# Four moves in a decoder trunk's order of work: first joint weights, weight sums, a shared sum, norm matmuls

## The chip, the cores and the metric

The kernel runs on one core of a Trainium2 chip, in one launch. The metric is device time in microseconds. Of the kernel before there are three timed runs, median 2136.77 (2134.54 to 2140.83), and one profiled execution, whose own time is 2129.51.

## The reference

Two decoder layers on `x[1, 1024, 1024]`, all in float32. Each layer is

```python
    for layer in range(DEPTH):
        h = _rmsnorm(x, pre_mix_g[layer])
        # layer 0: Conformer convolution and RG-LRU side by side; layer 1: mLSTM
        h = mixer(h)
        x = x + _rmsnorm(h, post_mix_g[layer])
        h = _swiglu(_rmsnorm(x, pre_ffn_g[layer]), w_gate[layer], w_up[layer], w_down[layer])
        x = x + _rmsnorm(h, post_ffn_g[layer])

def _swiglu(xn, w_gate, w_up, w_down):
    g = jnp.einsum('bsd,df->bsf', xn, w_gate)
    up = jnp.einsum('bsd,df->bsf', xn, w_up)
    return jnp.einsum('bsf,fd->bsd', jax.nn.silu(g) * up, w_down)
```

with a model width of 1024 and a feed-forward width of 2816 (22 blocks of 128). The Conformer branch of layer 0 holds a layer norm over 512 channels; two of its matmuls per half form the mean and the variance.

## The kernel before, in words

**Products.** To keep float32 accuracy, each operand is split in two float32r tiles, `hi` (a cast on ScalarE, L131) and `lo` (the rest, a subtraction on VectorE, L132), and each product is three matmuls: hi by hi, hi by lo, lo by hi (`mm3`, L125 to L128). A matmul has a 128x128 stationary tile and 512 moving columns. The sequence is worked on in two halves, A and B, of 512 rows.

**Feed-forward with seven products.** Class `Ffn` computes the two halves of both matrix products as a 2x2 block product in seven instead of eight block products, so it needs sums and differences of operand blocks. `phase0` and `down_first` (product d1) need half A alone. `phase1` does for each of 11 pairs of blocks `m` the products that need both halves: `pa`, `pb`, `pc`, each for gate and up. Their weights come from `prep1`: two loads of gate (`ri`, `rj`), two of up, four subtractions for each on GpSimd (L448 to L451: `t14`, `t23`), then the splits `t2.`, `t1.` and `b22`. The operands `s2`, `s3` are made from the features of half B (`feature_b`, names `xs2`, `xs3`), and a rest of twelve splits (`feature_c`: `xs1`, `xa22`, `xs4`) follows the first weights. `phase2` then does the products of `w_down`: d2, d3, d6, d5, d7 and a last one, each of 11 rounds (`down`); a round loads two 128x512 blocks into one raw tile, casts it (`whid`), subtracts (`wlod`) and issues 12 matmuls. The weights of d6 and of the products behind it are sums, made in `down_sums`: for each of the 11 pairs four loads (`wq`), four subtractions on GpSimd (`wt`) and four stores (`ft`).

**Sandwich.** After each mixer and feed-forward the residual step runs as a side generator (`sandwich`): for each of four row blocks a sum of squares, a power on GpSimd (`srp..`, `srn..`, L147), multiplications on VectorE (L214, L216), a store, and then the transposes that feed `feature_b`.

**What sets the order.** The code is a set of generators that are advanced in turn by given paces, and the list scheduler of the language then reorders the instructions of each engine; so where an edit lands is seen only in the order of the built program. Every engine works its own row of instructions in order. All loads and stores are issued by SyncE (SP), also in order: an issue that waits for a buffer holds the ones behind it. Buffers: 5 raw tiles shared by all weight loads, 4 `hi` and 4 `lo` tiles, 30 units, 13 small tiles, 8 banks of PSUM.

Names carry the layer and the pair: `whit200g` is the cast of `t2`, layer 0, pair 0, gate; `wlod0s31` is the subtraction of layer 0, product with `s3`, round 1. A number behind an underscore in an order row only numbers the tile.

Of the kernel before, what the change touches and what calls it, by code (L numbers as in the profile page):

```python
# [12 lines left out]
OP = mybir.AluOpType  # L13

P = 128
D = 1024
S = 1024
T = 512
NT = 4
# [21 lines left out]
def trunk(ctx: ExitStack, tc: tile.TileContext, x, w_in, w_out, w_gate, w_up, w_down,  # L41
# [18 lines left out]
    def ps_main(name):  # L60
        return pp.tile([P, T], F32, tag="mm", name=name, bufs=4)

    def ps_aux(shape, name):
        return pp.tile(shape, F32, tag="aux", name=name, bufs=4)
# [258 lines left out]
    TT = nc.vector.tensor_tensor  # L323

    class Ffn:
# [103 lines left out]
        def prep1(self, m):  # L429
            return self.prep1b(m, *self.prep1a(m))  # L430

        def prep1a(self, m):
            l = self.l
            sub = nc.gpsimd.tensor_tensor
            res = []
            raw = []
            for kind in range(2):
                name = f"{l}{m}{'gu'[kind]}"
                ri = raw_tile([P, D], f"ri{name}")
                rj = raw_tile([P, D], f"rj{name}")  # L440
                src = (w_gate, w_up)[kind]
                nc.sync.dma_start(ri, src[l, m])
                nc.sync.dma_start(rj, src[l, m + HP])
                u2 = small([P, T], f"u2{name}")
                nc.sync.dma_start(u2, self.d_p[m, kind])
                t23 = unit([P, 2, T], F32, f"t23{name}")
                t14 = unit([P, 2, T], F32, f"t14{name}")
                sub(t14[:, 0], rj[:, 0:T], ri[:, 0:T], op=OP.subtract)  # L448
                sub(t23[:, 0], rj[:, T:], t14[:, 0], op=OP.subtract)
                sub(t23[:, 1], rj[:, T:], rj[:, 0:T], op=OP.subtract)  # L450
                sub(t14[:, 1], ri[:, T:], t23[:, 0], op=OP.subtract)  # L451
                raw.append((rj, t23, t14))
                res.append({"u2": u2})
            for kind in range(2):
                u = unit([P, 2, T], F32R, f"b22{l}{m}{'gu'[kind]}")
                split(u[:, 0], u[:, 1], raw[kind][0][:, T:])
                res[kind]["b22"] = (u[:, 0], u[:, 1])
            return res, raw
# [13 lines left out]
        def phase1(self, ms):  # L472
            l = self.l
            ms = list(ms)
            w_next = self.prep1(ms[0])
            for _ in self.rest:
                pass
            for n, m in enumerate(ms):
                w, h11 = w_next
                u2 = [w[k]["u2"] for k in range(2)]  # L480
# [113 lines left out]
        def down_first(self):  # L594

            a = [ps_main(f"d1{self.l}{t}") for t in range(NT)]
            for _ in self.down(a, "a11", (0, 0), True):
                yield 2.8
            for t in range(NT):
                f = small([P, T], f"y1{self.l}{t}")  # L600
                nc.scalar.copy(f, a[t])
                nc.sync.dma_start(self.d_y[t], f)

        def phase2(self, oa, ob, by_t=False):
# [5 lines left out]
            u2 = [small([P, T], f"v2{l}{t}") for t in range(NT)]  # L610
            for t in range(NT):
                nc.sync.dma_start(u2[t], self.d_y[t])
            for _ in self.down_sums():
                pass
            a = [ps_main(f"d2{l}{t}") for t in range(NT)]
            for _ in self.down(a, "a12", (1, 0), True):
                yield 2.8
            for t in range(NT):
                TT(ya[t][:, lo], a[t], u2[t], op=OP.add)
            b = [ps_aux([P, T], f"d3{l}{t}") for t in range(NT)]  # L620
            for _ in self.down(b, "s4", (1, 1), True):
                yield 2.8
            for t in range(NT):
                nc.scalar.copy(ya[t][:, hi], b[t])  # L624
            a = [ps_main(f"d6{l}{t}") for t in range(NT)]
# [7 lines left out]
            for t in range(NT):  # L633
                nc.scalar.copy(yb[t][:, hi], b[t])
                TT(ya[t][:, hi], b[t], ya[t][:, hi], op=OP.add)
                TT(ya[t][:, hi], ya[t][:, hi], u2[t], op=OP.add)
                oa.ready = t
            a = [ps_main(f"d7{l}{t}") for t in range(NT)]
            for _ in self.down(a, "s3", "t3", True):
                yield 2.8  # L640
            for t in range(NT):
                TT(yb[t][:, hi], a[t], yb[t][:, hi], op=OP.add)
                TT(yb[t][:, hi], yb[t][:, hi], u2[t], op=OP.add)
            for t in self.down(a, "a22", "t4", False, by_t):
                if t is not None:
                    TT(yb[t][:, lo], a[t], u2[t], op=OP.add)
# [161 lines left out]
    def conformer(m):  # L808
# [16 lines left out]
        sq = [q[j // 2][:, j % 2] for j in range(4)]  # L825

        def mean(src, tmp, name):
            pm = ps_aux([P, T], name)
            nc.gpsimd.tensor_tensor(tmp[0], src[0], src[1], op=OP.add)
            nc.vector.tensor_tensor(tmp[2], src[2], src[3], op=OP.add)  # L830
            nc.vector.tensor_tensor(tmp[0], tmp[0], tmp[2], op=OP.add)
            nc.tensor.matmul(pm, onesl, tmp[0], start=True, stop=True)
            return pm

        pm = mean(acc, sq, f"pm{h}")
        yield
        for j in range(4):
            nc.vector.tensor_tensor(acc[j], acc[j], pm, op=OP.subtract)
            nc.scalar.activation(sq[j], acc[j], AF.Square)
            yield  # L840
        pv = mean(sq, sq, f"pv{h}")
        yield
        rs = sq[3]
        nc.scalar.activation(rs, pv, AF.Sqrt, bias=epsc)
        nc.vector.reciprocal(rs, rs)
# [378 lines left out]
    ob = Out("oB")  # L1224
    gb = start(sandwich(ob, x, x1, post_mix[0:1], 1, gf(0), f0.feature_b, 6), 1.0)
    run(Project(mb.yT, ob, OUT0).run())
    run(f0.phase0(LATE))
    run(f0.down_first())
    drain(gb)
# [22 lines left out]
    pb = Out("pB")  # L1252
    gb = start(sandwich(pb, x2, x3, post_mix[1:2], 1, gf(1), f1.feature_b, 6), 1.0)
    run(Project(nb.yT, pb, OUT1).run())
    run(f1.phase0(LATE))
    run(f1.down_first())
    drain(gb)
# [96 lines left out]
```

## Time and profile before

| what | value |
|---|---|
| median of three runs | 2136.77 us (2134.54 to 2140.83) |
| profiled execution, its own time | 2129.51 us |
| its span in the trace | 2127.7 us |
| mean granted clock of TensorE | 0.990 |
| TensorE (PE) busy | 2049.7 us, 96% |
| VectorE (DVE) busy | 1455.5 us, 68% |
| ScalarE (ACT) busy | 925.9 us, 44% |
| GpSimd (POOL) busy | 704.7 us, 33% |
| chain that ended last | PE 67%, DVE 13%, DMA 9%, issue 6%, ACT 4% |

The span runs from the first to the last instruction of the trace; the 1.8 us by which the time is longer lie around it. [...] Busy shares are means over the whole span: the stages differ, and each is to be read by itself.

### The profile page before, as it was taken

To read this page: it belongs to the slowest core of one execution; us is meant where nothing else is said; L and a number is where in the kernel's file an instruction comes from. 1 tells how busy PE (TensorE), PEld (TensorE's weight loads), DVE (VectorE), ACT (ScalarE), POOL (GpSimd) and SP (SyncE) were. 2 spreads that over 40 slices of the span, in tenths; PEclk is the share of its full clock that TensorE was granted. 3 is DMA by queue.
4 is the path that set the end of the run, shared out by engine and by line. 5 is a ranking of instruction groups with operands and counts; after the bars stand their busy time and mean duration, and the time that the engine had idled before them with its cause. 6 is when DMAs were issued, how large, how long until landed. Compare 5 with 4: busy or idle time off the path is not lost.

```text
span 2127.7 us, 26147 instructions
## 1 busy us (share of the span) xinstructions
PE 2049.7 (96%) x9200; PEld 1669.0 (78%) x9200; DVE 1455.5 (68%) x2017; ACT 925.9 (44%) x1313; POOL 704.7 (33%) x473
## 2 busy tenths in 40 slices
PE   7998989997999999999999999999997999999998
PEld 6776867785888887878988887778885888888786
DVE  7998479569677776567643755556469877777567
ACT  5666477654222222445343334555454222223353
POOL 4454554627444336401000000300016643445310
PEclk9999999998999999999999999999998999999999
DMA  6232544475454459966563653756464545469966
GB/s 229 92 117 81 182 163 163 144 248 187 164 167 160 168 201 366 342 203 229 190 208 118 219 180 99 257 179 213 134 223 176 192 167 168 165 214 367 327 225 220
DMA packets 202740, 417.39 MB, mean 196 GB/s; under 512 B 19920, under 2 KB 48720, under 8 KB 202608
## 3 DMA queue, kind: packets, MB, share of 16 engines
q1 hardware_dynamic: 202608, 415.72, 57.2%
q8 instruction: 72, 1.18, 0.2%
q14 instruction: 60, 0.49, 0.1%
HBM read 302.82 MB, written 112.82 MB: 195 GB/s over the span
## 4 chain that ended last, share of the span: by engine, by line
PE 67%; DVE 13%; DMA 9%; issue 6%; ACT 4%; POOL 1%; SPq 1%; DVEq 0%; POOLq 0%; ACTq 0%
PE pb L128 4%; PE pb L126 4%; PE pb L127 4%; PE pc L128 3%; PE pc L126 3%; PE pc L127 3%; DVE pcv L754 3%; PE d L126 3%; PE d L127 3%; PE d L128 3%; PE p L126 3%; PE p L127 3%; PE p L128 3%; DMA ft<-wt 2%; PE pa L128 2%
## 5 line engine op out<-in xcount | busy, mean ns | idle before, releaser
L107 ACT CAST whi<-raw 128x1024 fp32r<-128x1024 f32 (+2 forms) x164 | 164.3, 1006 | 244.2 <-PE p L127 50.0
L109 POOL TENSOR_TENSOR wlo<-raw,whi 128x1024 fp32r<-128x1024 f32 x66 | 162.0, 2461 | 165.8 <-ACT whi L107 126.5
L109 DVE TENSOR_TENSOR wlo<-raw,whi 128x1024 fp32r<-128x1024 f32 (+2 forms) x98 | 111.7, 1145 | 123.7 <-ACT whi L107 122.8
L754 DVE SCALAR_TENSOR_TENSOR pcv<-cy,vec,pcv 128x512 f32<-128x512 f32 x240 | 172.1, 749 | 4.4 <-ACT pcv L751 1.6
L1091 POOL TENSOR_TENSOR hrr<-hss,half 128x8 f32<-128x8 f32 x8 | 13.1, 1643 | 243.7 <-DVE hss L1089 243.7
L132 DVE TENSOR_TENSOR wlod1s<-r21s,whid1s 128x1024 fp32r<-128x1024 f32 x44 | 58.5, 1334 | 46.4 <-ACT whid1s L131 46.0
L132 DVE TENSOR_TENSOR wlod0s<-r20s,whid0s 128x1024 fp32r<-128x1024 f32 x44 | 57.6, 1310 | 44.0 <-ACT whid0s L131 39.8
L126 PE MATMUL p<-xTnoA,whi 128*128 128x512 f32 x176 | 71.8, 412 | 6.2 <-ACT gel L729 2.6
L131 ACT CAST whid1s<-r21s 128x1024 fp32r<-128x1024 f32 x44 | 46.4, 1054 | 66.7 <-PE d L128 38.0
L131 ACT CAST whid0s<-r20s 128x1024 fp32r<-128x1024 f32 x44 | 46.4, 1054 | 61.3 <-PE d L128 49.0
L127 PE MATMUL d<-wlod0s,whid0s 128*128 128x512 f32 x176 | 69.2, 393 | 2.0 <-DVE wlod0s L132 2.0
L126 PE MATMUL p<-xTnpA,whi 128*128 128x512 f32 x176 | 70.9, 405 | 0.0
L127 PE MATMUL p<-xTnoA,whi 128*128 128x512 f32 x176 | 70.3, 400 | 0.0
L128 PE MATMUL p<-xTnpA,wlo 128*128 128x512 f32 x176 | 70.3, 401 | 0.0
L127 PE MATMUL p<-xTnpA,whi 128*128 128x512 f32 x176 | 70.1, 399 | 0.0
L128 PE MATMUL p<-xTnoA,wlo 128*128 128x512 f32 x176 | 69.8, 400 | 0.0
L128 PE MATMUL d<-whid1s,wlod1s 128*128 128x512 f32 x176 | 69.1, 393 | 0.0
L127 PE MATMUL d<-wlod1s,whid1s 128*128 128x512 f32 x176 | 69.0, 392 | 0.0
L128 PE MATMUL d<-whid0s,wlod0s 128*128 128x512 f32 x176 | 68.6, 390 | 0.0
L126 PE MATMUL d<-whid1s 128*128 128x512 f32 x176 | 63.1, 394 | 3.1 <-ACT yeA L624 3.1
L132 DVE TENSOR_TENSOR wlod0a<-r20a,whid0a 128x1024 fp32r<-128x1024 f32 x33 | 47.3, 1440 | 25.3 <-ACT whid0a L131 23.8
L548 POOL TENSOR_TENSOR wt<-wq 128x512 f32<-128x512 f32 x22 | 34.7, 1575 | 89.0 <-DMA wq<-in_w_down 49.6
(2484 smaller groups left out, 6640.8 us busy)
## 6 DMA issues: line engine op xcount, KB each, us to landing
wq<-in_w_down SPq DMA_DIRECT2D x88, 256.0 KB, 5.1
ft<-wt SPq DMA_DIRECT2D x88, 256.0 KB, 5.1
raw<-in_w_in SPq DMA_DIRECT2D x32, 512.0 KB, 3.4
raw<-in_m_in SPq DMA_DIRECT2D x32, 512.0 KB, 4.9
raw<-in_w_gate SPq DMA_DIRECT2D x22, 512.0 KB, 4.5
raw<-in_w_up SPq DMA_DIRECT2D x22, 512.0 KB, 3.6
fp<-p1f SPq DMA_DIRECT2D x44, 256.0 KB, 2.5
fs<-s SPq DMA_DIRECT2D x44, 256.0 KB, 3.5
```

The source lines that it names most:

```text
L107: nc.scalar.copy(hi[:, 0:n], raw[:, 0:n])
L109: eng.tensor_tensor(lo[:, 0:n], raw[:, 0:n], hi[:, 0:n].bitcast(F32), op=OP.subtract)
L126: nc.tensor.matmul(ps, l[0], r[0], start=first, stop=False, **kw)
L127: nc.tensor.matmul(ps, l[0], r[1], start=False, stop=False, **kw)
L128: nc.tensor.matmul(ps, l[1], r[0], start=False, stop=last, **kw)
L131: nc.scalar.copy(dst_hi, src)
L132: nc.vector.tensor_tensor(dst_lo, src, dst_hi.bitcast(F32), op=OP.subtract)
L548: sub(t[0][:, 0], q[0][:, 1], q[0][:, 0], op=OP.subtract)
L754: nc.vector.scalar_tensor_tensor(dst, src[:, k:k + T], V(wname, w0 + k), dst, op0=OP.mult, op1=OP.add)
L1091: nc.gpsimd.tensor_tensor(rr, ss, half, op=OP.pow)
```

## The change

Four edits, in both layers except the last.

1. `prep1a` can be called for gate and up apart, and splits `b22` of each right away. The gate part of the first pair is called ahead of `phase0(LATE)`, that is ahead of the last first-half pair; the up part after the fourth round of `down_first`. `phase1` then only calls `prep1b` for it.
2. `phase2` no longer runs all of `down_sums` ahead of d2: one pair's sums are issued in every second round of d2 and d3, and the rest behind.
3. The add of the shared sum `u2` to the upper half of `yb` moves from behind product d7 to ahead of it.
4. In the layer norm of layer 0 the two `mean` matmuls of each half are emitted four steps of the generator later, after their sums.

```diff
-        def prep1a(self, m):
+        def prep1a(self, m, kinds=(0, 1), begun=None):
...
-            res = []
-            raw = []
-            for kind in range(2):
+            res, raw = begun or ([], [])
+            for kind in kinds:
...
                 res.append({"u2": u2})
-            for kind in range(2):
                 u = unit([P, 2, T], F32R, f"b22{l}{m}{'gu'[kind]}")
                 split(u[:, 0], u[:, 1], raw[kind][0][:, T:])
...
-            w_next = self.prep1(ms[0])
+            w_next = self.prep1b(ms[0], *self.begun)
...
-            for _ in self.down(a, "a11", (0, 0), True):
+            for i, _ in enumerate(self.down(a, "a11", (0, 0), True)):
                 yield 2.8
+                if i == 3:
+                    self.begun = self.prep1a(0, (1,), self.begun)
...
-            for _ in self.down_sums():
-                pass
+            sums = self.down_sums()
             a = [ps_main(f"d2{l}{t}") for t in range(NT)]
-            for _ in self.down(a, "a12", (1, 0), True):
+            for i, _ in enumerate(self.down(a, "a12", (1, 0), True)):
+                if i % 2 == 0:
+                    next(sums, None)
                 yield 2.8
...
-            for _ in self.down(b, "s4", (1, 1), True):
+            for i, _ in enumerate(self.down(b, "s4", (1, 1), True)):
+                if i % 2 == 0 or i == 9:
+                    next(sums, None)
                 yield 2.8
+            for _ in sums:
+                pass
...
                 oa.ready = t
+            for t in range(NT):
+                TT(yb[t][:, hi], yb[t][:, hi], u2[t], op=OP.add)
             a = [ps_main(f"d7{l}{t}") for t in range(NT)]
...
                 TT(yb[t][:, hi], a[t], yb[t][:, hi], op=OP.add)
-                TT(yb[t][:, hi], yb[t][:, hi], u2[t], op=OP.add)
...
         def mean(src, tmp, name):
-            pm = ps_aux([P, T], name)
...
+            for _ in range(4):
+                yield
+            pm = ps_aux([P, T], name)
             nc.tensor.matmul(pm, onesl, tmp[0], start=True, stop=True)
+            yield
             return pm
...
+    f0.begun = f0.prep1a(0, (0,))
     run(f0.phase0(LATE))
...
+    f1.begun = f1.prep1a(0, (0,))
     run(f1.phase0(LATE))
```

What the scheduler makes of it, at three places. First POOL's row in layer 0 around the last two row blocks of the sandwich (`srp`, `srn`) and the first pair's subtractions (`t14`, `t23`); before:

```order
L147 TENSOR_TENSOR srpoB2_3558<-svpoB2_3556,half_78 128x1
L147 TENSOR_TENSOR srnoB2_3582<-svnoB2_3580,half_78 128x1
L147 TENSOR_TENSOR srpoB3_3592<-svpoB3_3590,half_78 128x1
L147 TENSOR_TENSOR srnoB3_3630<-svnoB3_3628,half_78 128x1
L448 TENSOR_TENSOR t1400g_4021<-rj00g_4015,ri00g_4014 128x512
L450 TENSOR_TENSOR t2300g_4020<-rj00g_4015 128x512
L449 TENSOR_TENSOR t2300g_4020<-rj00g_4015,t1400g_4021 128x512
L448 TENSOR_TENSOR t1400u_4033<-rj00u_4027,ri00u_4026 128x512
L450 TENSOR_TENSOR t2300u_4032<-rj00u_4027 128x512
L451 TENSOR_TENSOR t1400g_4021<-ri00g_4014,t2300g_4020 128x512
```

and of the changed kernel:

```order
L147 TENSOR_TENSOR srpoB2_3558<-svpoB2_3556,half_78 128x1
L447 TENSOR_TENSOR t1400g_3602<-rj00g_3596,ri00g_3595 128x512
L449 TENSOR_TENSOR t2300g_3601<-rj00g_3596 128x512
L448 TENSOR_TENSOR t2300g_3601<-rj00g_3596,t1400g_3602 128x512
L147 TENSOR_TENSOR srnoB2_3582<-svnoB2_3580,half_78 128x1
L147 TENSOR_TENSOR srpoB3_3592<-svpoB3_3590,half_78 128x1
L450 TENSOR_TENSOR t1400g_3602<-ri00g_3595,t2300g_3601 128x512
L147 TENSOR_TENSOR srnoB3_3645<-svnoB3_3643,half_78 128x1
L447 TENSOR_TENSOR t1400u_3891<-rj00u_3885,ri00u_3884 128x512
L449 TENSOR_TENSOR t2300u_3890<-rj00u_3885 128x512
```

The gate subtractions moved in among the sandwich's powers, and the up subtractions follow the last power. Layer 1 has the same rows with `pB` for `oB`.

Second, DVE's row in `phase2` of layer 1, around the adds that read the product d2 (`d21.`, L619, in the changed kernel L620) among the splits of d3 (`s4`) and d6 (`s2`); before:

```order
L132 TENSOR_TENSOR wlod1s20_16142<-r21s20_16138,whid1s20_16141 128x1024
L132 TENSOR_TENSOR wlod1s21_16161<-r21s21_16157,whid1s21_16160 128x1024
L132 TENSOR_TENSOR wlod1s22_16180<-r21s22_16176,whid1s22_16179 128x1024
L132 TENSOR_TENSOR wlod1s23_16199<-r21s23_16195,whid1s23_16198 128x1024
L619 TENSOR_TENSOR yeA0_15508<-d210_15700,v210_15516 128x512
L619 TENSOR_TENSOR yeA1_15509<-d211_15701,v211_15517 128x512
```

and of the changed kernel:

```order
L132 TENSOR_TENSOR wlod1s40_15845<-r21s40_15841,whid1s40_15844 128x1024
L132 TENSOR_TENSOR wlod1s41_15880<-r21s41_15876,whid1s41_15879 128x1024
L620 TENSOR_TENSOR yeA0_15508<-d210_15524,v210_15516 128x512
L132 TENSOR_TENSOR wlod1s42_15899<-r21s42_15895,whid1s42_15898 128x1024
L620 TENSOR_TENSOR yeA1_15509<-d211_15525,v211_15517 128x512
```

The adds stood behind the fourth split of d6 and stand now behind the second of d3, 13 splits earlier.

Third, DVE's row in layer 0 between the products d5 and d7 (`d50.` is d5's sum, `v20.` the shared sum); before:

```order
L635 TENSOR_TENSOR yfA0_6316<-d500_7163,yfA0_6316 128x512
L635 TENSOR_TENSOR yfA1_6317<-d501_7164,yfA1_6317 128x512
L635 TENSOR_TENSOR yfA2_6318<-d502_7165,yfA2_6318 128x512
L636 TENSOR_TENSOR yfA0_6316<-yfA0_6316,v200_6324 128x512
L635 TENSOR_TENSOR yfA3_6319<-d503_7166,yfA3_6319 128x512
L636 TENSOR_TENSOR yfA1_6317<-yfA1_6317,v201_6325 128x512
L636 TENSOR_TENSOR yfA2_6318<-yfA2_6318,v202_6326 128x512
L132 TENSOR_TENSOR wlod0s31_7425<-r20s31_7421,whid0s31_7424 128x1024
```

and of the changed kernel:

```order
L640 TENSOR_TENSOR yfA0_6316<-d500_7163,yfA0_6316 128x512
L644 TENSOR_TENSOR yfB0_6320<-yfB0_6320,v200_6324 128x512
L640 TENSOR_TENSOR yfA1_6317<-d501_7164,yfA1_6317 128x512
L644 TENSOR_TENSOR yfB1_6321<-yfB1_6321,v201_6325 128x512
L640 TENSOR_TENSOR yfA2_6318<-d502_7165,yfA2_6318 128x512
L644 TENSOR_TENSOR yfB2_6322<-yfB2_6322,v202_6326 128x512
L641 TENSOR_TENSOR yfA0_6316<-yfA0_6316,v200_6324 128x512
L640 TENSOR_TENSOR yfA3_6319<-d503_7166,yfA3_6319 128x512
L644 TENSOR_TENSOR yfB3_6323<-yfB3_6323,v203_6327 128x512
L641 TENSOR_TENSOR yfA1_6317<-yfA1_6317,v201_6325 128x512
L132 TENSOR_TENSOR wlod0s31_7429<-r20s31_7425,whid0s31_7428 128x1024
```

Seven adds stood ahead of the split of the second round of d7, and ten stand there now.

## Rows read from the trace of the kernel before

**Rows 1.** The page, busy us, share of the span, instructions.

```profile
PE 2049.7 (96%) x9200; PEld 1669.0 (78%) x9200; DVE 1455.5 (68%) x2017; ACT 925.9 (44%) x1313; POOL 704.7 (33%) x473
```

**Rows 2.** PE's waits, whole span: us in total, times, longest us.

```profile
PE pa L126 <- ACT whit210g L131: 9.2, 1, 9.2
PE d L127 <- DVE wlod0a L132: 8.5, 5, 4.8
```

**Rows 3.** Busy us by stretch: stretch, us, engines, granted clock, DMA share, GB/s.

```profile
485.00:515.00 30.00, 17.70 (x52) 12.40 (x51) 29.69 (x29) 14.65 (x25) 21.00 (x12) 0.77 0.47 163
818.00:842.00 24.00, 20.71 (x83) 16.18 (x82) 14.35 (x10) 6.99 (x7) 12.99 (x9) 0.93 1.05 400
...
942.00:960.00 18.00, 16.03 (x70) 12.15 (x69) 16.57 (x24) 10.99 (x15) 5.59 (x4) 1.00 0.71 238
...
1608.00:1637.00 29.00, 16.95 (x53) 11.95 (x52) 28.14 (x30) 18.06 (x30) 14.67 (x9) 0.76 0.39 137
1992.00:2002.00 10.00, 6.91 (x24) 5.28 (x23) 5.44 (x7) 4.18 (x8) 6.50 (x4) 0.83 1.04 392
```

**Rows 4.** DVE timeline, layer 0: start us, us, engine, line, instruction [idle before].

```profile
480.68 0.69 DVE L384 TENSOR_TENSOR xanoB<-xsnoB,xanoB 128x512 f32<-128x512 f32 x1
...
483.53 1.77 DVE L388 TENSOR_TENSOR xknoB<-xknoB,xanoB 128x512 f32<-128x512 f32 x1
...
496.46 0.68 DVE L132 TENSOR_TENSOR xs2noB<-xanoB,xs2noB 128x512 fp32r<-128x512 f32 x1
...
497.97 1.23 DVE L132 TENSOR_TENSOR wlot200g<-t2300g,whit200g 128x1024 fp32r<-128x1024 f32 x1 [0.24 <-ACT whit200g L131]
499.12 0.69 DVE L132 TENSOR_TENSOR b2200g<-rj00g,b2200g 128x512 fp32r<-128x512 f32 x1
...
510.80 2.33 DVE L132 TENSOR_TENSOR wlot200u<-t2300u,whit200u 128x1024 fp32r<-128x1024 f32 x1
```

**Rows 5.** POOL timeline, layer 0, the first pair's first subtraction.

```profile
480.70 1.83 POOL L448 TENSOR_TENSOR t1400g<-rj00g,ri00g 128x512 f32<-128x512 f32 x1 [18.76 <-DMA rj00g<-in_w_gate]
```

**Rows 6.** Busy us by stretch (PE, PEld, DVE, ACT, POOL), ahead of the features.

```profile
450.00:465.00 15.00, 15.00 (x72) 12.30 (x71) 10.62 (x14) 10.29 (x13) 3.35 (x4) 1.00 1.00 357
...
1570.00:1592.00 22.00, 22.00 (x106) 17.93 (x105) 14.70 (x19) 15.56 (x22) 3.53 (x5) 1.00 0.96 320
```

**Rows 7.** DVE timeline, layer 1, start of `phase1`.

```profile
1619.73 1.23 DVE L132 TENSOR_TENSOR wlot210g<-t2310g,whit210g 128x1024 fp32r<-128x1024 f32 x1 [0.66 <-ACT whit210g L131]
...
1632.55 2.31 DVE L132 TENSOR_TENSOR wlot210u<-t2310u,whit210u 128x1024 fp32r<-128x1024 f32 x1
```

**Rows 8.** PE timeline around the norm's second matmul, first half.

```profile
173.07 0.40 PE L126 MATMUL pia<-xTb,whi 128*128 128x512 f32 x1
173.31 0.40 PE L127 MATMUL pia<-xTb,whi 128*128 128x512 f32 x1
177.67 1.18 PE L832 MATMUL pv<-lnq,onesl 128*128 128x512 f32 x2 [3.97 <-DVE lnq L831]
...
179.08 0.63 PE L126 MATMUL pia<-xTb,whi 128*128 128x512 f32 x1
179.51 0.63 PE L127 MATMUL pia<-xTb,whi 128*128 128x512 f32 x1
```

**Rows 9.** PE's waits from 795 to 1000, `phase2` of layer 0.

```profile
PE d L127 <- DVE wlod0a L132: 3.7, 4, 2.2
...
PE d L126 <- DVE yfA L619: 1.3, 1, 1.3
```

**Rows 10.** Timelines of DVE and PE, layer 1, start of product d6.

```profile
1995.26 1.22 DVE L132 TENSOR_TENSOR wlod1s<-r21s,whid1s 128x1024 fp32r<-128x1024 f32 x1 [1.48 <-ACT whid1s L131]
1996.40 2.48 DVE L619 TENSOR_TENSOR yeA<-d,v 128x512 f32<-128x512 f32 x4
...
1997.23 0.47 PE L126 MATMUL d<-whid1s 128*128 128x512 f32 x1 [3.09 <-ACT yeA L624]
```

**Rows 11.** Timelines of DVE and PE, layer 0, start of product d7.

```profile
942.14 0.68 DVE L636 TENSOR_TENSOR yfA<-yfA,v 128x512 f32<-128x512 f32 x1
942.74 0.68 DVE L635 TENSOR_TENSOR yfA<-d,yfA 128x512 f32<-128x512 f32 x1
...
945.82 0.50 PE L127 MATMUL d<-wlod0s,whid0s 128*128 128x512 f32 x1 [1.39 <-DVE wlod0s L132]
```

More of the change, by code (lines that the diff above doesn't have):

```diff
@@ L831, in mean @@
             nc.vector.tensor_tensor(tmp[0], tmp[0], tmp[2], op=OP.add)
+            for _ in range(4):
+                yield
+            pm = ps_aux([P, T], name)
             nc.tensor.matmul(pm, onesl, tmp[0], start=True, stop=True)
+            yield
             return pm
-        pm = mean(acc, sq, f"pm{h}")
-        yield
+        pm = yield from mean(acc, sq, f"pm{h}")
         for j in range(4):
@@ L840, in conformer @@
             yield
-        pv = mean(sq, sq, f"pv{h}")
-        yield
+        pv = yield from mean(sq, sq, f"pv{h}")
         rs = sq[3]
```

## The prediction

> **What bounds the kernel now.** I read the page's busy times first, then the list of what TensorE (PE) waited for, then busy times by stretch, then the timelines of single engines. PE is busy for 96% of the span [rows 1], so a change in the order of work can only win PE's idle time and the stretches in which PE runs at its lower clock. The list of waits says where that time is [rows 2]: 9.2 us before the first joint product of layer 1 (`pa`, which waits for the cast `whit210g`), 4.8 us at once for `wlod0a`, at the end of layer 0's first `down` product. Both belong to one place that occurs once per layer, the start of `phase1`. There PE is busy for 17.7 us of 30 in layer 0 and for 16.95 of 29 in layer 1, at a mean granted clock of 0.77 and 0.76, while VectorE (DVE) is busy for 29.7 of 30 and 28.1 of 29 [rows 3]. So DVE sets the end of that stage, not PE.
>
> Why DVE is late there shows in its timeline [rows 4]: a 128x512 subtraction takes 0.69 us at 480.68 and 1.77 us at 483.53, with nothing changed but that GpSimd (POOL) began the weight subtractions of the first pair at 480.70 [rows 5]. That is 1.05 us lost on DVE for each of the eight POOL subtractions, 8.4 us per layer. DVE then finishes the last second-product operand at 497.1 (496.46 + 0.68; I call this moment T0) and `wlot200u`, the last thing the second `pa` product needs, at 513.1 (T_w): 16.0 us for `wlot200g`, two splits of `b22`, twelve operand splits and `wlot200u`. In layer 1 `wlot210g` waits 0.66 us for its cast and starts at 1619.73, and `wlot210u` ends at 1634.9 [rows 7].
>
> **The change part by part.** The sum is made on the profiled execution, 2129.51 us with a span of 2127.7.
>
> *Norm.* In PE's order only one matmul moves: `pv` of the first half goes behind four matmuls of the block that it stood in. It waits for DVE until 177.67 either way, and PE idles 3.97 us in front of it [rows 8]. Four matmuls at 0.24 us apart (173.07 to 173.31) fill 0.9 of that: -0.9. At best the lower clock that follows (0.43 us from 179.08 to 179.51) goes too, some 1.7; at worst nothing is won.
>
> *First pair, layer 0.* POOL's four gate subtractions move to behind `srpoB2`, three of them ahead of `srnoB2` and `srpoB3`; the up subtractions follow `srnoB3`, in the middle of the first `down` product. SP issues the gate loads right behind the last weight loads, ahead of the loads of the `down` product, the up loads behind the product's fourth round. Terms for T0: the contention of 481 to 497 goes, -8.4. Three gate subtractions now meet the sandwich's DVE work around 451 to 456, whose last row leads to the features: +3.1 (three of 1.05, less a little), and `b2200g`, a 128x512 split, stands ahead of it: +0.7. DVE is free for 4.4 us of 15 there [rows 6], but most of that lies behind the place. The four up subtractions meet features, which run without a break: +4.2. `wlot200g` now stands ahead of T0: +1.2. Together T0 comes 0.8 later. From T0 to T_w, `wlot200g`, `b2200g` and a wait of 0.24 are gone [rows 4]: -2.1. But `u200g`, which reads the first `pa` product, now stands ahead of all twelve splits, so DVE waits for PE, and everything behind it with it: PE has 3 of the 12 matmuls left when T0 comes, or all of them and the last `down` round. I take 1.0; at the lower clock it would be 12 x 0.43 = 5.2 less the 1.2 us of work that DVE still has, 4.0. Sum: -0.3. Range: -8.4, if POOL's work hides wholly in DVE's free time, to +3.
>
> *First pair, layer 1.* The same order, but DVE has more room: 7.3 us free of 22 from 1570 to 1592 [rows 6], where the gate and half of the up subtractions land. I charge half of each: -8.4 + 2.1 + 2.1 + 1.2 + 0.7 = -2.3 for T0. Behind T0 go `wlot210g`, `b2210g` and the wait of 0.66, and 1.0 is added by the same wait on PE: -1.6. `whit210g` also no longer stands behind the copies of the `down` product on ScalarE (ACT). Sum: -3.9; range -9 to +2.
>
> The row decides what contention costs: 0.69 against 1.77 us. [...]
>
> *Weight sums over two products.* From 795 to 1000 PE waits 3.7 us for `wlod0a`, up to 2.2 at a time, and once 1.3 us for L619 [rows 9]; in layer 1 it waits 3.1 us, ending when the first L619 add is done at 1997.1, an add that stands on DVE behind a split which waits for ACT and a load [rows 10]. (The list names ACT's L624; the times say L619.) The DMA share is 1.05 at that place in layer 0 and 1.04 in layer 1 [rows 3]: the sums' loads and stores fill it. With the change L619 stands right behind the first two splits of the next product, in layer 1 13 splits earlier, and the product that it reads has long ended by then. So its two waits go: 1.3 + 3.1, and the lower clock behind the second, 10 x 0.17 = 1.7 [rows 3]: -6.1. The waits for `wlod0a` (3.7, and 24 x 0.07 = 1.7 of lower clock) come from loads late on a full DMA; they now stand ahead of the sums' loads on SP, but the DMA is as full, so I take half: -2.7. Sum: -8.8, range -11.5 to 0. The sums end later on SP by up to 14 DMAs; the sixth product's loads run rounds ahead, and that covers it unless they fall a whole product behind.
>
> *Shared sum ahead.* Four adds of 0.68 us (some 0.6 apart) move from behind the `d7` product, where PE is fed by work already split, to ahead of it. Ten adds instead of seven stand ahead of `wlod0s31`, for which PE already waits 1.39 us at 945.82 [rows 11]: +1.8, less 0.2 of a later small wait: +1.6. In layer 1 PE does not wait there: 0 to +1, taken as 0. Range 0 to +3.5: the wait would be 3.2 us, and one of 3.1 was followed by 0.83 of full clock, one of 1.39 by 1.00 [rows 3]. [...]
>
> **Sum.** -0.9 - 0.3 - 3.9 - 8.8 + 1.6 = -12.3, so 2117.2 for the profiled execution. That execution was 7.3 us faster than the median of the runs, 2136.77; the difference applied to the median gives 2124.5.
>
> **Rivals.**
> *The contention only moves.* Every POOL subtraction finds two-input work on DVE, so the stage ends where it did in both layers. For it: layer 0, where DVE is nearly full on both sides. Against it: the free time in layer 1. -0.9 - 8.8 + 1.6 = -8.1: 2128.7.
> *The first pair gets through free.* The loads come early, POOL is done before the features start in both layers, and T_w moves by the whole 8.4 twice: -0.9 - 16.8 - 8.8 + 1.6 = -24.9: 2111.9. Against it: the up loads are held back to the middle of `down`.
> *Phase 2 stays bound by the DMA.* Share 1.05 whatever the order; waits only change rows, and the gain of that part is nil: -0.9 - 4.2 + 1.6 = -3.5: 2133.3.
> *The sums block the loads (slower).* SP issues in order. A sum's load waits for a buffer that POOL frees, and now one stands ahead of the loads of every second round in both products, not bunched. If each of the eleven sums holds the round behind it long enough for a wait of 1.1 us, half of the longest seen, both layers lose 12.1 instead of winning 8.8: -0.9 - 4.2 + 24.2 + 1.6 = +20.7: 2157.5. It decides where a sum waits longer than the rounds that are split ahead (four buffers, some 11 us at 2.8 a round). Against it: in the order, loads mostly pass the sums.
>
> **How the numbers follow.** Forecast 0.52 (its own range 2117 to 2131), contention only moves 0.21, free 0.11, DMA-bound 0.09, slower 0.07. Under 0.3% (6.4 us) this kernel cannot be told from no change. Faster by more, below 2130.4: nearly all of the forecast (0.49), 0.13 of the first rival, 0.11, a little of the third: 0.74. Within: 0.18. Slower: 0.08. The range 2110 to 2134 leaves out the slower rival and the tails.
>
> **What would show it.** Right: no wait for the L619 adds in either layer; the wait for `whit210g` down from 9.2 to some 5 us; DVE's 128x512 work at 1.7 us beside the sandwich and at 0.69 where the last features are; a wait near 3 us for `wlod0s31`. Wrong: POOL's first subtractions still beside features at full cost with T_w unmoved; a wait on DVE in front of `u200g` of 4 us; new waits for `wlod0s` or `wlod1s` in rounds behind a sum; any time below 2110 or above 2134.

## The result and the profile after

The changed kernel takes 2126.86 us (median of 6 runs, 2119.88 to 2128.55), the kernel before 2137.16 beside it (6 runs, 2134.07 to 2140.83): a ratio of 0.9946 [0.9927, 0.9965], 10.3 us less, where 12.3 were forecast. The profiled execution took 2119.88 us, where 2117.2 were forecast, with a span of 2118.1. From its page, the lines that answer to [rows 1], and the chain that ended last:

```profile
PE 2047.9 (97%) x9200; PEld 1666.6 (79%) x9200; DVE 1459.9 (69%) x2017; ACT 926.7 (44%) x1314; POOL 715.0 (34%) x473
...
PE 73%; DVE 9%; DMA 7%; issue 5%; ACT 4%; POOL 1%; SPq 0%; DVEq 0%; POOLq 0%; ACTq 0%
```

The work is the same; what changed is what PE waits for. Its waits over the whole span (total us, times, longest), to hold against [rows 2] and [rows 9]:

```profile
PE pa L126 <- ACT whit210u L131: 6.8, 1, 6.8
PE pa L126 <- ACT whit200u L131: 5.1, 1, 5.1
PE d L127 <- DVE wlod0s L132: 4.2, 2, 3.2
PE d L126 <- ACT whid0s L131: 3.6, 2, 3.3
PE d L126 <- ACT whid0a L131: 3.1, 1, 3.1
...
PE d L127 <- DVE wlod0a L132: 2.2, 3, 1.4
```

The wait of 9.2 us for `whit210g` is gone, those for `wlod0a` fell from 8.5 to 2.2, and no wait for the L619 adds (now L620) is left. (Of the 8.5, a single wait of 4.8 at the end of layer 0's d1 stands in this profile of before alone: the runs of the other three edits alone, further down, had 3.8 to 5.3 in all and none above 1.6.) In their place stand waits for casts of the *up* half, `whit200u` and `whit210u`, and waits in the middle of d1 (`whid0a`), in the last round of d6 (`whid0s`) and in the second round of d7 (`wlod0s`), all of layer 0. The stretches that answer to [rows 3] (PE, PEld, DVE, ACT, POOL busy, clock, DMA share, GB/s):

```profile
478.00:508.00 30.00, 23.57 (x94) 18.63 (x94) 29.08 (x38) 21.96 (x35) 9.01 (x4) 0.89 0.60 201
815.00:839.00 24.00, 23.46 (x102) 18.64 (x101) 13.86 (x11) 9.31 (x9) 9.47 (x6) 1.00 1.03 369
936.00:954.00 18.00, 14.69 (x58) 11.31 (x57) 15.75 (x22) 7.68 (x10) 4.18 (x3) 0.91 0.57 180
1600.00:1630.00 30.00, 22.68 (x88) 17.68 (x87) 28.80 (x39) 20.17 (x34) 11.20 (x4) 0.83 0.51 174
1983.00:1993.00 10.00, 10.00 (x46) 8.29 (x45) 5.13 (x4) 5.99 (x8) 5.58 (x5) 1.00 1.05 389
```

At the two starts of `phase1` PE is busy for 23.6 and 22.7 us of 30 instead of 17.7 of 30 and 16.95 of 29, at a higher clock. At the place of the old L619 wait in layer 1 it is busy for 10 of 10. Of these five only d7 (936 to 954) got worse: 14.69 against 16.03, the clock at 0.91 against 1.00.

Every kernel here issues 9200 matmuls, nearly all in the same order, so a stage can be timed between the starts of the matmuls with the same numbers in each trace. Means over the profiled executions of this study without an edit and with it (experiments that touch the same stage in another way left out; in brackets how many executions):

```
stage                            without        with    difference   predicted
norm, last first-half pair         27.8 (5)     26.9 (6)  -0.9         -0.9
d1 and first pair, layer 0         72.1 (4)     69.3 (5)  -2.8         -0.3
d1 and first pair, layer 1         65.5 (4)     62.8 (5)  -2.7         -3.9
d2, d3, d6, d5, layer 0           126.7 (6)    123.6 (4)  -3.1  }
d2, d3, start of d6, layer 1       73.5 (6)     68.1 (4)  -5.4  }      -8.8
from there to the end             114.3 (6)    116.3 (4)  +2.0  }
d7, layer 0                        62.2 (7)     64.8 (3)  +2.6         +1.6
sum                                                      -10.3        -12.3
```

In the norm's stretch PE waits 2.7 us for `pm` in some executions and 6.3 in others, of whatever kernel. The first row has those with 6.3; where it is 2.7, as in both profiles of before and after, 25.8 became 23.4.

Most rows repeat closely: the first pair of layer 1 within 0.5 us, d7 of layer 0 within 1.1. Two rows of layer 0 do not. D1 and the first pair took 71.1 to 72.8 without the edit and 66.6 to 70.9 with it, and d2 to d5 took 122.8 to 130.5 without and 123.1 to 123.9 with it. In the latter the two sets overlap, the profile of before being the quickest of all, so the -3.1 is a mean and not a difference that each pair of executions shows.

### The profile page after: what moved, and what is told of

The parts are those of the page before. It is cut to its first block, busy times and chain, and to the rows that moved or that the text cites. A ratio compares the mean times of both kernels' runs of the same rounds, so it can differ in the third digit from the quotient of the medians.

```text
span 2118.1 us, 26124 instructions
## 1 busy us (share of the span) xinstructions
PE 2047.9 (97%) x9200; PEld 1666.6 (79%) x9200; DVE 1459.9 (69%) x2017; ACT 926.7 (44%) x1314; POOL 715.0 (34%) x473
## 3 DMA queue, kind: packets, MB, share of 16 engines
q1 hardware_dynamic: 202608, 415.72, 57.7%
## 4 chain that ended last, share of the span: by engine, by line
PE 73%; DVE 9%; DMA 7%; issue 5%; ACT 4%; POOL 1%; SPq 0%; DVEq 0%; POOLq 0%; ACTq 0%
PE d L127 4%; PE d L128 4%; PE d L126 4%; PE pb L126 4%; PE pb L128 4%; PE pb L127 4%; PE pc L128 4%; PE pc L127 4%; PE pc L126 4%; PE p L126 3%; PE p L127 3%; DVE pcv L760 3%; PE p L128 3%; PE pa L126 2%; PE pa L127 2%
## 5 line engine op out<-in xcount | busy, mean ns | idle before, releaser
L126 PE MATMUL p<-xTnoA,whi 128*128 128x512 f32 x176 | 71.1, 408 | 6.2 <-ACT gel L735 2.6
L131 ACT CAST whid0s<-r20s 128x1024 fp32r<-128x1024 f32 x44 | 46.2, 1053 | 67.9 <-PE d L128 57.4
L127 PE MATMUL p<-xTnpA,whi 128*128 128x512 f32 x176 | 70.9, 403 | 0.0
L128 PE MATMUL d<-whid0s,wlod0s 128*128 128x512 f32 x176 | 69.8, 397 | 0.0
L126 PE MATMUL d<-whid1s 128*128 128x512 f32 x176 | 61.2, 390 | 0.7 <-ACT whid1s L131 0.7
```

Source lines behind the costliest of these rows:

```text
L126: nc.tensor.matmul(ps, l[0], r[0], start=first, stop=False, **kw)
L127: nc.tensor.matmul(ps, l[0], r[1], start=False, stop=False, **kw)
L128: nc.tensor.matmul(ps, l[1], r[0], start=False, stop=last, **kw)
L131: nc.scalar.copy(dst_hi, src)
```

## The experiments

**Each part alone.** Four kernels are the kernel before with one part of the change.

*The norm.*

```diff
+            for _ in range(4):
+                yield
+            pm = ps_aux([P, T], name)
```

> The kernel before with edit 4 alone (norm's matmuls four steps behind). Theory, from the two traces: the wait in front of the first half's pv matmul falls from 3.97 us to some 1.5, and with it part of the stretch at the lower clock, -2 to -3 us. Rival, the prediction's term: four matmuls fill 0.9 of the wait, -0.9 us, the rest of the difference seen between the traces came from elsewhere. Both: no other wait of PE changes by more than 0.5 us.

Measured 2134.6, ratio 0.9988 [0.9979, 0.9998]. In its profiled execution PE waits 6.3 us for `pm` and 1.1 for `pv`, where the kernels without the edit have 1.4 to 2.0 for `pv` beside a `pm` wait of 6.3; the stage is 0.9 shorter, as the rival had it.

*The first pair.*

```diff
+                if i == 3:
+                    self.begun = self.prep1a(0, (1,), self.begun)
...
+    f0.begun = f0.prep1a(0, (0,))
...
+    f1.begun = f1.prep1a(0, (0,))
```

> The kernel before with edit 1 alone (first joint weights begun ahead). Theory: DVE is relieved at the start of phase1 (T_w 5 to 8 us earlier in both layers), but the up loads go in front of the first down product's loads on a full DMA, so PE waits some 3 to 5 us in d1 of layer 0 and 1 to 2 in layer 1; net -2.5 to -3 us per layer, -5 to -6 in all. Rival, the prediction's terms: -0.3 in layer 0 and -3.9 in layer 1 with no wait in d1.

Measured 2134.22, 0.9989 [0.9980, 0.9999], which is -2.0 and less than both expectations. The waits in d1 came (1.1 for `whid0a` and 3.1 for `wlod0a` in layer 0). By stages this execution wins 5.5 in layer 0 (66.6 against 72.1) and 2.5 in layer 1, but its d2 to d5 of layer 0 take 130.5, the longest of all, with a wait of 3.7 us for the L619 adds instead of 1.3. Whether the earlier first pair causes that is not shown.

*The sums.*

```diff
-            for _ in self.down_sums():
-                pass
...
+                if i % 2 == 0:
+                    next(sums, None)
```

> The kernel before with edit 2 alone (weight sums spread over two products). Theory: the waits for wlod0a and for the L619 adds go (-5 to -6 us in layer 0, -4 to -5 in layer 1), but the last sum ends so late that the last round of d6 in layer 0 waits some 3 us for its load, with a stretch at the lower clock behind it: layer 0 nets -1 to +1, all -3.5 to -5.5. Rival, the prediction's term: -8.8, no wait in d6; then the wait in d6 seen in the changed kernel comes from the other edits.

Measured 2129.69, 0.9973 [0.9964, 0.9982]: -6.6. PE waits 3.1 us for `whid0s` in d6 here too, so that wait belongs to this edit and not to the others.

*The shared sum.*

```diff
+            for t in range(NT):
+                TT(yb[t][:, hi], yb[t][:, hi], u2[t], op=OP.add)
...
-                TT(yb[t][:, hi], yb[t][:, hi], u2[t], op=OP.add)
```

> The kernel before with edit 3 alone (shared sum added ahead of d7). Theory: the wait for wlod0s31 in layer 0 grows from 1.39 to 3.2 us and the lower clock follows it, +3 to +3.5 us. Rival, the prediction's term: +1.6, no stretch at the lower clock. Both: layer 1 unchanged within 0.5 us.

Measured 2137.2, 1.0006 [0.9995, 1.0017]. The wait for `wlod0s` is 3.2 us here too, and d7 takes 64.9 instead of 62.2; the whole time shows neither the +3 of the theory nor the +1.6 of its rival clearly.

Against the 2136.26 of before, run beside them, the four make -1.7, -2.0, -6.6 and +0.9, together -9.4, and the whole change made -10.3: the parts add up, within about 2 us of uncertainty for each. The sums carry two thirds, and the shared sum wins nothing. The first pair's -2.0 is less than the -5.5 that its two stages show in the table, by the d2 to d5 just named.

**The change without the shared sum.** The two hunks on `yb` undone:

```diff
-            for t in range(NT):
-                TT(yb[t][:, hi], yb[t][:, hi], u2[t], op=OP.add)
...
+                TT(yb[t][:, hi], yb[t][:, hi], u2[t], op=OP.add)
```

> The changed kernel without edit 3 (shared sum added behind d7, as before). Theory: the wait for wlod0s31 in layer 0 falls from 3.2 to 1.4 us and the lower clock behind it goes: -2 to -3.5 against the changed kernel, 0.993 of before. Rival (the adds behind d7 cost as much where they stood): no difference from the changed kernel.

Measured 2125.52, 0.9945 [0.9928, 0.9963]. By the whole time it can't be told from the change (0.9946), where -2 to -3.5 were expected. By the stage it can: d7 takes 62.1 us without the part, 64.6 with it. The timelines of DVE and PE after, to hold against [rows 11]:

```profile
939.75 1.22 DVE L132 TENSOR_TENSOR wlod0s<-r20s,whid0s 128x1024 fp32r<-128x1024 f32 x1
...
941.02 0.50 PE L127 MATMUL d<-wlod0s,whid0s 128*128 128x512 f32 x1 [3.20 <-DVE wlod0s L132]
941.36 0.40 PE L128 MATMUL d<-whid0s,wlod0s 128*128 128x512 f32 x1
...
941.94 0.63 PE L128 MATMUL d<-whid0s,wlod0s 128*128 128x512 f32 x1
```

The wait for `wlod0s` grew from 1.39 to 3.20 us, and from 0.9 us after its end the matmuls take 0.63 instead of 0.40: the lower clock followed, 0.50 from 942 to 944, where [rows 3] had 1.00 from 942 to 960.

**What the contention costs.** The kernel before, in which POOL does none of the first pair's eight subtractions per layer: `t14` and `t23` are filled straight from memory, so the combination of the first pair's weights is left out.

```diff
+                if m == 0:
+                    rj = t23.rearrange("p a b -> p (a b)")
+                    nc.sync.dma_start(t14.rearrange("p a b -> p (a b)"), src[l, m])
+                    nc.sync.dma_start(rj, src[l, m + HP])
```

> The kernel before, in which the first pair's eight GpSimd subtractions per layer are left out: the weights are loaded straight into t14 and t23, as many bytes as before, so the values are not the reference's. Theory (DVE is late at the start of phase1 because GpSimd's subtractions slow it by 1.05 us each): DVE's 128x512 subtractions at 481 to 497 us fall back from 1.77 to 0.69 us, T0 comes 7 to 8.4 us earlier in each layer and the first pa product with it; the time falls by 8 to 16 us, which bounds what edit 1 can ever win. Rival (the stage waits for ScalarE's casts, the loads or PE's own work): DVE is faster there but the first pa product moves by less than 3 us per layer, and the time by less than 5.

Measured 2133.52, 0.9988 [0.9975, 1.0002]. DVE in layer 0, and ACT behind it:

```profile
488.95 0.69 DVE L388 TENSOR_TENSOR xknoB<-xknoB,xanoB 128x512 f32<-128x512 f32 x1
490.09 0.69 DVE L132 TENSOR_TENSOR xs2noB<-xanoB,xs2noB 128x512 fp32r<-128x512 f32 x1 [0.45 <-ACT xs2noB L131]
...
496.87 0.62 ACT L131 CAST b2200g<-t2300g 128x512 fp32r<-128x512 f32 x1 [5.31 <-DMA t2300g<-in_w_gate]
```

Without POOL's work the subtraction that took 1.77 us in [rows 4] takes 0.69. T0 comes at 490.8 instead of 497.1, and counted from the first matmul of d1 7.9 us earlier in layer 0 and 6.7 in layer 1. So the cause of the slow DVE is shown. The time does not follow in full: the loads into `t23` land late, and PE waits 8.7 and 8.0 us for the casts `whit200g` and `whit210g`. Layer 0's first pair wins nothing (72.8), layer 1's 4 to 6 us (59 to 61 against 65.5, by where the stage is cut). As a bound on what the contention is worth the run is inconclusive.

**Where the up half is begun.** The change, with the up loads and subtractions back at the start of `phase1`:

```diff
-                if i == 3:
-                    self.begun = self.prep1a(0, (1,), self.begun)
...
+            self.begun = self.prep1a(0, (1,), self.begun)
             w_next = self.prep1b(ms[0], *self.begun)
```

> The changed kernel with the up half of the first pair begun at the start of phase1 again, the gate half still ahead. Theory (the up loads crowd the first down product's loads on a full DMA): PE's wait of 3.1 us for whid0a in d1 of layer 0 falls under 1, and those of 0.9 and 0.9 in layer 1 go, but the four up subtractions slow DVE again where the last features are, T_w 3 to 5 us later per layer; against the changed kernel +1 to +4, so 0.996 to 0.997 of before. Rival (the raw tiles that the gate half holds starve d1): the wait in d1 stays at 3 us. Second rival (contention does not count): time falls 4 to 5 us under the changed kernel.

Measured 2129.31, 0.9966 [0.9952, 0.9979], inside the expected range, though the interval overlaps that of the change. PE's waits, and DVE and PE at the end of layer 0's d1:

```profile
PE pa L126 <- ACT whit210u L131: 6.8, 1, 6.8
...
PE pa L126 <- ACT y L600: 5.2, 1, 5.2
```

```profile
479.32 2.32 DVE L132 TENSOR_TENSOR wlod0a<-r20a,whid0a 128x1024 fp32r<-128x1024 f32 x1
...
487.44 0.77 PE L127 MATMUL d<-wlod0a,whid0a 128*128 128x512 f32 x1 [2.68 <-DVE wlod0a L132]
```

The 3.1 us in front of d1's `whid0a` go, but the wait moves more than it vanishes: beside the up subtractions DVE is slow again at the end of d1 (2.32 us for `wlod0a`, where others of the same work take some 1.22), and PE waits 2.7 us for `wlod0a` there. In all PE waits 4.4 us in d1 of layer 0, against 4.9 in the changed kernel. So layer 0 ends its stage where it did (68.7 against 69.0), and layer 1 loses 2.1 (65.0 against 62.9), where the 5.2 us for `y` are new. The wait for `whit210u` stays at 6.8 whether its data is early or late: the data does not set it.

**One sum in every round of d2.**

```diff
-                if i % 2 == 0:
-                    next(sums, None)
+                next(sums, None)
```

> The changed kernel with one pair's sums in every round of d2 instead of every second round of d2 and d3; in the order the last sum is then issued as early as before, and the L619 adds stand as late as before. Theory (the late last sum makes d6's last round in layer 0 wait): that wait of 3.3 us and the lower clock behind it go, -4 to -5; the waits for the L619 adds come back, +1.3 in layer 0 and +4.8 in layer 1; wlod0a in d2 waits under 1 us; against the changed kernel -1 to +2. Rival (the DMA is full whatever the order): the d6 wait goes but as much returns as waits for wlod0a in d2 and d3 of layer 0.

Measured 2138.82, 1.0007 [0.9996, 1.0019]: the whole gain of that part and more is gone, 12 us against the changed kernel, where -1 to +2 were expected. PE's waits:

```profile
PE d L126 <- DVE yeA L619: 3.9, 1, 3.9
PE d L126 <- DVE yfA L619: 3.9, 1, 3.9
```

In the timeline of DVE the first L619 adds of layer 1 stand behind the last of a row of splits again:

```profile
2007.07 2.09 DVE L132 TENSOR_TENSOR wlod1s<-r21s,whid1s 128x1024 fp32r<-128x1024 f32 x1 [1.48 <-ACT whid1s L131]
2009.08 1.27 DVE L619 TENSOR_TENSOR yeA<-d,v 128x512 f32<-128x512 f32 x2
```

In the changed kernel the same adds (L620) start as soon as PE has ended the product that they read, some 35 us earlier (52.5 by the two timelines, of which 17 are the lead that the changed kernel has by then):

```profile
1956.58 0.69 DVE L620 TENSOR_TENSOR yeA<-d,v 128x512 f32<-128x512 f32 x1 [1.09 <-PE d L128]
```

So in layer 1 this part wins by the place that the scheduler gives these adds: with a sum in every round the wait is back, and d2, d3 and the start of d6 take as long as without the edit (73.7 against 72.8 to 74.2, and 68.1 in the changed kernel). In layer 0 the wait for d6's last loads went as expected (`whid0s` 0.5), but the L619 wait of 3.9 is longer than in the profile of before (1.3), and d2 and d3 took 4 us longer than in the changed kernel as well.

**A pace in between,** without the shared sum:

```diff
-                if i % 2 == 0:
+                if i in (0, 1, 2, 4, 6, 8, 10):
...
-                if i % 2 == 0 or i == 9:
+                if i in (0, 2, 4, 6):
```

> The changed kernel without edit 3 and with the sums three rounds earlier (rounds 0, 1, 2, 4, 6, 8, 10 of d2 and 0, 2, 4, 6 of d3); the L619 adds stand as early as in the changed kernel. Theory: d6's wait for its last loads in layer 0 (2.3 to 3.3 us) falls under 1 and the lower clock behind it goes, with no wait for the L619 adds; -3 to -5 against the run without edit 3 alone, 0.992 to 0.993 of before. Rival (the full DMA delays some round in any order): the d6 wait shrinks, and 2 us or more appear as waits for wlod0a in d2 of layer 0.

Measured 2121.55, 0.9940 [0.9926, 0.9954], which the whole time does not tell from the 0.9945 of the slower pace. By stages d6 and d5 of layer 0 fall from 66.2 to 62.4 and the stretch to the end from 116.4 to 114.2, but d2 and d3 of layer 0 took 61.8 instead of 57.7 in this execution; in the next two kernels, with the same pace, they take 57.5 and 57.4. The wait in d6 fell to 1.6, not under 1, and 3.1 us of waits for `whid0a` and `wlod0a` stand in d2 and d3, as the rival had it.

**The rest splits later.** `self.rest` is the twelve operand splits (`xs1`, `xa22`, `xs4`) that `phase1` issues ahead of its products. First in the kernel before:

```diff
-            for _ in self.rest:
-                pass
...
                     w_next = self.prep1(ms[n + 1])
+                if n == 0:
+                    for _ in range(3):
+                        next(self.rest, None)
```

> The kernel before with nothing but the twelve rest splits of the features emitted behind the next pair's preparation, so that whit200u and wlot200u stand ahead of them on ScalarE and VectorE. Theory (what PE waits for in the middle of phase1's start is the second half's cast, queued behind the twelve rest splits): PE's waits behind the first pa product (whit200u, wlot200u, whit210u: 2.8 to 5 us each) go, -3 to -5 us per layer, 0.996 of before. Rival (VectorE's throughput under GpSimd's contention sets the end of the stage, whatever the order): the waits move to the pc and second pb products and the time falls by less than 2 us.

Measured 2139.69, 1.0024 [1.0013, 1.0035]: a loss. PE's waits:

```profile
PE pa L126 <- ACT whit210g L131: 9.2, 1, 9.2
...
PE pc L127 <- DVE xs1noB L132: 3.3, 3, 2.1
```

`whit210g` does not stand behind the rest splits, so its 9.2 us stay, and `xs1` is now late as well. The waits for `whit200u`, `wlot200u` and `whit210u` went, as expected. The first pair of layer 0 wins 2.8 (69.3 against 72.1) and that of layer 1 3.4 (62.1 against 65.5), and the rest of `phase1` in layer 1 gives back 4.5 (283.1 against 278.6). These stages do not account for the whole loss of 5.1; in this execution the L619 wait in layer 0 is 3.6 and d2 to d5 take 128.5, and the remainder was not found. Then the same edit on top of the kernel with the pace in between:

> The run c1 with the twelve rest splits behind the next pair's preparation too. Theory: PE's waits of 5.1 us (whit200u) and 6.8 us (whit210u) go, T_w comes 6 to 8 us earlier, and the stage ends where VectorE has done the rest splits: -6 to -10 against c1, 0.988 to 0.990 of before. Rival (VectorE's throughput): the wait moves to the pc product of the first pair, less than -3.

Measured 2117.25, 0.9921 [0.9908, 0.9933], 4.3 less than the run before it, where 6 to 10 were expected. The waits for `whit200u` and `whit210u` are gone, layer 1's first pair takes 57.6 us instead of 62.9. Layer 0's wins nothing (69.8 against 68.9): T0 comes 3.8 us later there, and PE waits for `xs2` and `xs1`. At last, with the up half begun behind the first round of d1:

```diff
-                if i == 3:
+                if i == 0:
```

> The run best3 with the up half begun after the first round of the down product instead of the fourth. Theory (the loads of the up half meet the fullest DMA share there): the wait for whid0a in d1 of layer 0 stays at 3 us or grows by 1 to 3; in layer 1 the up cast now stands ahead of the last features, -1 to -2; against best3 0 to +2. Rival: the earlier subtractions relieve VectorE at the features, -2 to -4 against best3.

Measured 2113.56 (2112.68 to 2114.85), 0.9905 [0.9890, 0.9919]: faster than both kernels, and 3.7 less than the run before it, as the rival had it. The first pair wins 1.1 in layer 0 and 1.8 in layer 1; in d1 of layer 0 PE waits 1.6 us for `whid0a`, not 3. Its stretch at the start of `phase1` in layer 1, and its longest waits at the start of `phase1`:

```profile
1600.00:1635.00 35.00, 30.84 (x130) 23.70 (x129) 34.93 (x40) 21.93 (x34) 19.28 (x9) 1.00 0.68 231
```

```profile
PE pa L126 <- ACT y L602: 2.5, 1, 2.5
PE pc L128 <- DVE wlot100g L132: 2.4, 1, 2.4
```

DVE is busy for all of it, yet PE works for 88% of the stretch at the full clock, where the changed kernel had 76% at 0.83. So here a busy DVE by itself did not hold PE back; what differs between the two kernels is the order.

## Why the prediction was right, and where it was not

**The norm, -0.9.** Right in kind: -0.9 in executions with the long `pm` wait. The term was worked out on an execution with the short one, though, and there it was -2.4: `pv` waits 1.5 us instead of 4.0 [rows 8], and the matmuls behind it take 0.39 us instead of 0.63. That is the term's best case, in which the lower clock goes too (1.00 from 172 to 182); that its middle figure fits the other executions is partly luck.

**The first pair, layer 0, -0.3.** Under-sized: -2.8. Two terms were off. The stage starts at 450.5 (455.3 before) by its first matmul; counted from there T0 came 2.7 us later (forecast 0.8), and the way from T0 to T_w fell from 16.0 to 10.2 us (forecast 1.1 less). DVE after, to hold against [rows 4]:

```profile
456.21 2.33 DVE L216 SCALAR_TENSOR_TENSOR xroB<-yoB,srpoB,xroB 128x1024 f32<-128x1024 f32 x1
...
483.70 0.69 DVE L384 TENSOR_TENSOR xanoB<-xsnoB,xanoB 128x512 f32<-128x512 f32 x1
...
493.23 1.76 DVE L132 TENSOR_TENSOR xs2noB<-xanoB,xs2noB 128x512 fp32r<-128x512 f32 x1
...
496.12 0.68 DVE L483 TENSOR_TENSOR u200g<-pa,u200g 128x512 f32<-128x512 f32 x1
496.72 2.48 DVE L132 TENSOR_TENSOR xs1noB<-xsnoB,xs1noB 128x512 fp32r<-128x512 f32 x4
...
501.54 2.48 DVE L132 TENSOR_TENSOR xs4noB<-xknoB,xs4noB 128x512 fp32r<-128x512 f32 x4
503.95 1.21 DVE L132 TENSOR_TENSOR wlot200u<-t2300u,whit200u 128x1024 fp32r<-128x1024 f32 x1
```

The contention moved into the sandwich, as forecast: 128x1024 work takes 2.3 us there, the middle features are back at 0.69. What the prediction had as a wait on DVE in front of `u200g` did not come (no idle time at 496.12). And it left out the second pair's subtractions: `xs4` takes 2.48 instead of 5.14 (at 505.74 before, beside a POOL subtraction from 507.04 on) and `wlot200u` 1.21 instead of 2.33, which are 3.8 of the 4.7 us that the forecast missed behind T0; the wait on PE that did not come is 1.0 more. A subtraction of the second pair stands beside these splits after the change too, but there POOL is slow and DVE is not (4.58 us where most take 1.3 to 2.3):

```profile
502.36 4.58 POOL L448 TENSOR_TENSOR t2301g<-rj01g,t1401g 128x512 f32<-128x512 f32 x1 [7.91 <-DVE xs4noB L132]
```

So a POOL subtraction does not always cost DVE the 1.1 us, though the prediction's first rival took that for granted; what decides who pays, no run shows.

Late is T0 in every execution with the edit: 42.4 to 45.8 us behind the start of d1, against 40.6 to 41.8 without, and the stage's length follows it (66.6 at the earliest T0, 70.9 at the latest). Part of it, in the changed kernel, are waits in d1, in POOL's, ACT's and PE's timelines:

```profile
464.00 1.29 POOL L447 TENSOR_TENSOR t1400u<-rj00u,ri00u 128x512 f32<-128x512 f32 x1 [3.46 <-DMA rj00u<-in_w_up]
...
468.43 1.04 ACT L131 CAST whid0a<-r20a 128x1024 fp32r<-128x1024 f32 x1 [3.65 <-DMA r20a<-in_w_down]
469.53 1.20 PE L126 MATMUL d<-whid0a 128*128 128x512 f32 x4 [3.14 <-ACT whid0a L131]
...
492.72 1.73 POOL L450 TENSOR_TENSOR t1400u<-ri00u,t2300u 128x512 f32<-128x512 f32 x1
```

The up loads stand on SP ahead of d1's next rounds, and PE waits 3.1 us for `whid0a` until the load of its round has landed. The prediction priced the up half's subtractions, not its loads; moving it back took that wait away, but put one of 2.7 us for `wlod0a` at the end of d1. Whether the transfers themselves delay that load or the raw tiles that they hold, no run separates. The fourth up subtraction falls behind one of the second pair, and both meet the last features.

**The first pair, layer 1, -3.9.** Over-sized: -2.7. T0 came 0.9 earlier (forecast 2.3) and T_w 7.1 earlier (forecast 3.9), more than forecast, but T_w no longer sets the end. ACT and PE:

```profile
1619.21 2.17 ACT L131 CAST xs4npB<-xknpB 128x512 fp32r<-128x512 f32 x4
1621.29 1.04 ACT L131 CAST whit210u<-t2310u 128x1024 fp32r<-128x1024 f32 x1
1622.38 0.80 PE L126 MATMUL pa<-xs2npB,whit210u 128*128 128x512 f32 x1 [6.77 <-ACT whit210u L131]
```

The cast for which PE waits 6.77 us starts right behind the rest splits on ACT (`xs4` is the last four of them). The forecast of a wait for `whit210g` of some 5 us did not come true: that wait is gone, and a new one took its place, in ACT's row. The sentence that failed is "DVE sets the end of that stage". With the weights early it is the order on ACT, twelve splits (1615.05 to 1621.38, without a pause) ahead of a cast that PE needs first; moving them won 5.3 us in layer 1 (62.9 to 57.6), where in the kernel before the same edit lost over the whole time.

**The sums, -8.8.** The mechanism is right, the size -6.5. The L619 waits went in both layers, and phase 2's waits for `wlod0a` fell from 3.7 us [rows 9] to 0.5. But the cover named for the later end of the sums, that the sixth product's loads run rounds ahead, failed. The chain that ended last, layer 0, after:

```profile
867.26 5.13 DMA wq<-in_w_down
872.40 5.14 DMA r20s<-ft
877.56 5.21 DMA wq<-in_w_down
882.84 3.37 DMA r20s<-fs
886.21 1.29 POOL wt L550
887.50 2.00 POOL wt L552
889.49 4.39 DMA ft<-wt
893.95 4.43 DMA r20s<-ft
898.54 1.05 ACT whid0s L131
899.64 2.92 PE d L126 x8
```

From 867 to 899 the end is set by loads of the last sum, its store and the load that reads it back, with d6's own loads between them; PE waits 3.3 us, and the clock falls (0.69 from 899.5 to 905). That is the third rival in one place: d6 and d5 take 66.2 to 66.8 us where four of the six executions without the edit took 61.2 to 62.2 (the other two, 67.1 and 67.2, had an L619 wait of 3.6 and 3.7), while d2 and d3 win about 6 (56.4 to 57.7 against a mean of 63.1). In layer 1 the late sums cost the 2.0 us to the end: `whid1s` waits of up to 1.2 us, which the kernel before does not have. The pace in between gives both back; one sum a round gives back the gain itself. The rival by which the sums block d2 and d3 did not occur at the change's pace, but a wait for `whid0s` behind a sum did, in kind one of the prediction's signs of being wrong (which named `wlod0s`). The profile of before, on which the term was made, was a quick one: its 122.8 us from d2 to d5 are the least of six.

**The shared sum, +1.6.** Right in kind, +2.6 in size. The wait came out at 3.20, as its range had it, and the lower clock followed (0.50 from 942 to 944), for which the middle figure had nothing.

**The sum.** Layer 0's first pair won 2.5 us more than forecast, and layer 1's, the sums and the shared sum made 1.2, 2.3 and 1.0 less; that 12.3 came so near to 10.3 is partly these cancelling. The whole time, 7.5 to 15.6 us less by its interval, rules out the rivals of -24.9, -3.5 and +20.7, but not the first, -8.1. That one is answered by the stages: its condition was that the start of `phase1` ends where it did, and T_w came 3.1 us earlier in layer 0 and 7.1 in layer 1.

## What to carry to other kernels

When a late operand is made early, look at once for what stands in front of its next use on the engine that prepares it: here another 5.3 us in layer 1 came when the splits ahead of that cast moved too, and over the whole time each of the two moves was worth little or less than nothing alone. A load that is moved earlier is also a load in front of somebody (here PE waited 3.1 us for `whid0a`): price its place on the queue beside its work. And work that is spread to fill gaps has a last piece, with a consumer behind it (here `whid0s`, a wait of 3.3 us); find that consumer before choosing the pace.

## What the runs showed of the hardware

Beside a POOL subtraction of 128x512, DVE's two-input work in several rows took about 1.1 us longer at both sizes: 0.69 became 1.76 us for 128x512, and 1.21 became 2.33 for 128x1024. It is not always DVE that pays: from 502.36 on in the changed kernel POOL's own subtraction took 4.58 us while DVE's splits beside it kept their 2.48 for four, and from 1622.18 on 7.43 beside splits of 2.49 for four and 1.22 for one of 128x1024. Elsewhere POOL's mostly took from 1.3 to 2.3 us.

In the changed kernel waits of 3.1 us (`whid0a`), 3.2 (`wlod0s`, in front of d7) and 3.3 (`whid0s`, in d6) were each followed by a lower clock, 0.73 from 469.5 to 472, 0.50 from 942 to 944 and 0.69 from 899.5 to 905, with 0.63 us for a matmul; one of 1.39 in the kernel before [rows 11] was not, with 0.39 to 0.50 us for a matmul behind it and a clock of 1.00 from 942 to 960. In front of d7 the lower clock came 0.9 us after PE had started again, as its timeline shows (0.40 at 941.36, 0.63 from 941.94 to 943.64). At a granted clock of 1.00 (946 to 948 there) matmuls started 0.23 us apart, at 0.50 (942 to 944) 0.43.
